# Squares through PSUM, FFN 0's and FFN 1's first superblock in a pinned order, and an own place for the forget bias

## The chip, the cores and the metric

The kernel runs on one core of a Trainium2 chip. The metric is device time in microseconds (us): the median of several executions, smaller is better. Besides the executions that are only timed, one is profiled; the rows shown are from that one. The engines are named as the profile names them: PE (TensorE, the matrix products), DVE (VectorE), ACT (ScalarE), POOL (GpSimd) and SP (SyncE, whose queue issues the DMAs). L276 is line 276 of the kernel before.

## The reference

One step of a two-layer encoder over 1024 prompt frames and 64 sample frames (T = 1088 columns here), with caches of 256 frames. Layer 0 mixes with two kinds of attention (A, B), layer 1 with a forgetting attention (C) and a recurrent branch (D); each layer ends in a SwiGLU feed-forward net.

```python
for layer in range(DEPTH):
    hp = rmsnorm(yp, norm_mix_g[layer])
    mp = ab_mixer(...) if layer % 2 == 0 else cd_mixer(...)
    yp = yp + mp
    yp = yp + swiglu(rmsnorm(yp, norm_ffn_g[layer]), w1, w3, w2)   # (silu(h @ w1) * (h @ w3)) @ w2
y = rmsnorm(yp, final_g)

def rmsnorm(x, g):
    return x * lax.rsqrt(jnp.mean(x * x, axis=-1, keepdims=True) + EPS) * g

def cd_mixer(...):                     # in part
    logf = log_sigmoid(cf + c_f_bias)
    F = jnp.cumsum(logf, axis=1)       # the forget bias of fox_core
    s = q @ k + F[query] - F[key]      # softmax, then times v
    u = causal_conv(dx); h = rg_lru(u) # recurrent branch, out = h * gelu(dg)
```

The same is computed for the sample frames, with the caches in front.

## The kernel before

All data are float32. A product is made of three matmuls on parts of the operands, high x high, high x low and low x high; `split` (L218) makes the parts: ACT copies the high part (L219), DVE or POOL subtracts it for the low part (L220). Activations lie transposed, 128 features on the partitions and the 1088 columns in three chunks (384, 384, 320). On chip there is one array `arena`, addressed by offsets whose names begin with F_, one array `split_arena` for split operands, and `banks`, the eight PSUM banks of 512 columns, which rings hand out in turn.

The engines' programs are static. The order on each engine is set by a scheduler that takes the instructions in the order of the code and weighs what is ready; `issue_after(x)` makes an instruction stand behind x. Each engine runs its list in order, and one that waits holds up all that are behind it. The stages that matter here:

*The output projection (`wout`, L824).* Per chunk, pairs of feature rows are multiplied (L248), added to x on DVE (L850), and squared into a running sum for the norm: `addsq` (L268) squares on ACT (L276) into a small buffer of the arena and adds on DVE (L277). `rms` (L252) multiplies the sum by a matrix of 1/1024 on PE (L258), and ACT takes the root as exp(-0.5 ln). `norm_x` (L906) scales eight rows per chunk on DVE (L910). The steps of `fill_x` (L917), lists `one` and `two` for the two halves of the columns, then make the sums and differences (L944) and the split operands of the feed-forward net, on ACT and DVE.

*The first products of the feed-forward net (`ffn`, L1049; `superblock`, L1012).* A superblock is a 2x2 block product in seven products (as Strassen does it) of 24 matmuls (L1028); there are 22 superblocks. Superblock 0 runs in two rounds, one for each half of the columns, with 12 matmuls a product. `left` (L969) makes the weight side: four adds on POOL (L982 to L985) and seven splits. ACT copies one product out of its bank (L1032) and computes Silu (L1090); DVE adds products (L1036, L1038, L1089).

*The second products and the tail.* Products L1128 to L1130, added to x (L1165), squared through `addsq`; here the adds of the squares go to DVE and POOL in turn. Weights are split on POOL.

*Layer CD (`recurrent`, L1385).* For four blocks m of the recurrent branch: products, a convolution on DVE (L1309, L1311), gates (L1334 to L1337), Gelu (L1293 to L1301) and the scan of the recurrence (`d_close`, L1339: POOL L1349, then ACT, then DVE), stored to `o_spill`. Between them lie the products of the first query heads (`put_q`, L321: ACT L324 and L325, DVE L329) and keys. `forget` (L1237) sums the log forget values with two scans on DVE (L1244) and stores them to `forget_rows`. Later `bias_c` (L761) loads one row of it to all partitions and POOL adds a mask (L765; L741 adds masks to pieces); the attention's first steps (L472) add it to the scores (L460, L461).

## Time and profile before

| | before |
|---|---|
| median of 3 runs | 2751.93 us (2747.84 to 2753.0) |
| the profiled execution | 2753.34 us |
| its span, first to last instruction | 2751.6 us |
| mean granted clock of TensorE | 0.976 |

A row of a timeline gives the start and the length in us, the engine, the line, what is written and read, and in square brackets how long the engine had stood idle before it and whom it waited for. A row of the waits names who waited for whom, how long in all, how often and the longest. The granted clock is a share of full speed.

### The profile page before, as it was taken

How to read it: one execution, taken by the hardware profiler on the slowest of the kernel's cores; microseconds unless marked ns; L12 is line 12 of the kernel's file. 1: busy time of each engine (PE TensorE's matmuls, PEld its weight loads, DVE VectorE, ACT ScalarE, POOL GpSimd, SP SyncE). 2: the span in 40 equal slices, each digit the busy share in tenths (PEclk: the TensorE clock that was granted, in tenths of full speed). 3: DMA queues.
4: the chain of work that ended last, by engine and by line, in shares of the span. 5: the costliest groups of instructions: out<-in, count | busy, mean ns of one | idle time of the engine just before them, and what ended most of it. 6: DMA issues, size and time to landing. Idle time of an engine off the chain costs nothing. (4 is left out here: it accounts for less than half of the span.)

```text
span 2751.6 us, 45123 instructions
## 1 busy us (share of the span) xinstructions
PE 2614.3 (95%) x17614; PEld 2541.5 (92%) x17614; DVE 1353.8 (49%) x2741; ACT 1209.4 (44%) x2384; POOL 1223.8 (44%) x968
## 2 busy tenths in 40 slices
PE   6999999989899999999998979998989999999997
PEld 5899999888899999999988979988989999999997
DVE  7666666667432332422156657777753233242214
ACT  5666667764323233311145566776432323331113
POOL 5222222323766676421364433343377666642123
PEclk9999999999999999999999989999989999999998
DMA  6222222352222212442242442244222222243213
GB/s 204 71 68 78 68 65 61 107 160 68 79 87 79 87 63 87 148 141 71 65 128 49 51 94 75 77 126 157 79 80 100 65 87 68 82 162 127 71 48 106
DMA packets 116407, 253.75 MB, mean 92 GB/s; under 512 B 21577, under 2 KB 70993, under 8 KB 116193
## 3 DMA queue, kind: packets, MB, share of 16 engines
q1 hardware_dynamic: 116192, 250.87, 30.0%
q8 instruction: 138, 2.26, 0.3%
q14 instruction: 77, 0.62, 0.1%
HBM read 182.63 MB, written 65.43 MB: 90 GB/s over the span
## 5 line engine op out<-in xcount | busy, mean ns | idle before, releaser
L220 POOL TENSOR_TENSOR split_arena<-arena,split_arena 128x512 fp32r<-128x512 f32 (+5 forms) x510 | 798.1, 1569 | 1196.9 <-ACT split_arena L219 1121.6
L1028 PE MATMUL banks<-split_arena 128*128 128x272 f32 x7392 | 947.5, 291 | 29.0 <-DVE split_arena L220 12.1
L1028 PEld LDWEIGHTS banks<-split_arena 128*128 128x128 f32 x7392 | 941.8, 191 | 34.1 <-DVE split_arena L220 13.5
L219 ACT ACTIVATE split_arena<-arena 128x512 fp32r<-128x512 f32 (+8 forms) x673 | 469.9, 710 | 1054.2 <-PE banks L1028 439.5
L248 PE MATMUL banks<-split_arena 128*128 128x384 f32 (+1 forms) x3384 | 641.3, 336 | 5.6 <-ACT arena L1337 3.1
L248 PEld LDWEIGHTS banks<-split_arena 128*128 128x128 f32 x3384 | 565.4, 192 | 13.7 <-ACT arena L1337 3.4
L1128 PE MATMUL banks<-split_arena 128*128 128x384 f32 (+1 forms) x1056 | 347.0, 329 | 6.3 <-DVE arena L1095 4.3
L1130 PE MATMUL banks<-split_arena 128*128 128x384 f32 (+1 forms) x1056 | 346.8, 329 | 5.9 <-POOL split_arena L220 5.9
L1129 PE MATMUL banks<-split_arena 128*128 128x384 f32 (+1 forms) x1056 | 346.5, 328 | 0.0
L220 DVE TENSOR_TENSOR split_arena<-banks,split_arena 128x512 fp32r<-128x512 f32 (+4 forms) x312 | 167.4, 541 | 95.7 <-ACT split_arena L219 92.9
L1128 PEld LDWEIGHTS banks<-split_arena 128*128 128x128 f32 x1056 | 199.9, 189 | 7.5 <-issue 3.8
L1130 PEld LDWEIGHTS banks<-split_arena 128*128 128x128 f32 x1056 | 200.0, 189 | 7.1 <-POOL split_arena L220 7.1
L472 DVE CUSTOM_DVE_ANT_0 arena<-banks,arena 128x384 f32<-128x384 f32 (+4 forms) x368 | 175.3, 493 | 56.6 <-PE banks L461 38.4
L1129 PEld LDWEIGHTS banks<-split_arena 128*128 128x128 f32 x1056 | 200.0, 189 | 0.5 <-DVE split_arena L220 0.2
L220 DVE TENSOR_TENSOR split_arena<-arena,split_arena 128x1088 fp32r<-128x1088 f32 (+8 forms) x163 | 161.4, 1001 | 76.8 <-ACT split_arena L219 76.0
L219 ACT ACTIVATE split_arena<-banks 128x512 fp32r<-128x512 f32 (+4 forms) x312 | 146.8, 477 | 98.5 <-PE banks L577 46.0
L1036 DVE TENSOR_TENSOR arena<-banks,arena 128x544 f32<-128x544 f32 (+1 forms) x46 | 32.0, 698 | 300.3 <-PE banks L1028 300.3
L474 ACT ACTIVATE arena<-arena 128x640 f32<-128x640 f32 (+8 forms) x216 | 156.3, 724 | 53.1 <-DVE arena L472 51.7
L1147 DVE TENSOR_TENSOR arena<-banks,arena 128x384 f32<-128x384 f32 (+1 forms) x96 | 51.3, 534 | 258.5 <-PE banks L1130 258.3
L577 PE MATMUL banks<-arena 128*128 128x128 f32 (+2 forms) x828 | 135.1, 275 | 16.6 <-DVE arena L493 10.1
L577 PEld LDWEIGHTS banks<-arena 128*128 128x128 f32 (+2 forms) x828 | 96.4, 141 | 34.6 <-DVE arena L493 13.6
L236 PE MATMUL banks<-split_arena 128*128 128x384 f32 (+1 forms) x312 | 107.2, 345 | 16.2 <-DVE split_arena L329 9.6
(165 smaller groups left out, 3128.7 us busy)
## 6 DMA issues: line engine op xcount, KB each, us to landing
arena<-in_w_dram SPq DMA_DIRECT2D x120, 512.0 KB, 3.5
h_spill<-arena SPq DMA_DIRECT2D x22, 1088.0 KB, 4.2
arena<-h_spill SPq DMA_DIRECT2D x44, 544.0 KB, 4.8
arena<-in_abw_dram SPq DMA_DIRECT2D x24, 512.0 KB, 3.9
arena<-in_w_dram SPq DMA_DIRECT2D x28, 384.0 KB, 3.2
arena<-in_cdw_dram SPq DMA_DIRECT2D x20, 512.0 KB, 3.8
x_spill<-arena SPq DMA_DIRECT2D x48, 192.0 KB, 2.3
arena<-x_spill SPq DMA_DIRECT2D x16, 544.0 KB, 4.6
```

The source lines that it names most:

```text
L219: self.nc.scalar.activation(hi, x, AF.Copy)
L220: return sub.tensor_tensor(lo, x, hi.bitcast(F32), op=ALU.subtract)
L236: nc.tensor.matmul(ps, wh[:, k], hh[k][:, c0:c0 + n], start=(k == ks[0]), stop=False)
L248: self.pe = self.nc.tensor.matmul(ps, x[:, k], y[k][:, c0:c0 + n], start=a and i == 0, stop=z and i == 2).ins
L472: nc.vector.tensor_tensor_reduce(o, p, t, -1.0, low, ALU.add, ALU.min, to)
L474: nc.scalar.activation(sb, sb, AF.Exp, bias=st[:, 0:1], scale=-1.0, accum_out=st[:, 1:2])
L577: nc.tensor.transpose(pt[:r, t * nq + s * m:t * nq + s * m + m], src, self.ident[:m, :m])
L1028: nc.tensor.matmul(bank[:, p], l[:, k], r[:, k, x], start=first and i == 0, stop=k == 3 and i == 2, skip_group_check=True)
L1128: nc.tensor.matmul(ps, wh, h[:, c0:c0 + n], start=j == j0, stop=False)
L1129: nc.tensor.matmul(ps, wh, lo[:, c0:c0 + n], start=False, stop=False)
L1130: nc.tensor.matmul(ps, wl, h[:, c0:c0 + n], start=False, stop=j == j1 - 1)
L1147: nc.vector.tensor_tensor(xs, ps, xs, op=ALU.add)
```

## The change

It has five parts.

1. For chunks 1 and 2 of `wout`, and in the feed-forward net's tail, the squares go to a PSUM bank, and all adds are DVE's. In the tail the last chunk no longer has two running sums, so its mean square is one matmul instead of two.
2. `norm_x(0)` is issued behind the first pair of products of chunk 1.
3. The mean square and scaling of chunk 2 and the last steps of `fill_x` move into superblock 0 (`rest` behind the third product of round 1, `last` behind the seventh). The products of superblock 0 stand in a pinned order, 0, 2, 1, 3, 4, 5, 6 in each round; Silu in it comes behind the root of the mean square. The weights of superblock 1 are loaded later, and `left(1)` may be issued only behind the high part of the last fill.
4. The log forget values have a place of their own (F_LF) instead of two slots of the recurrent branch, and `forget` stands behind the convolution of m = 1 in the code.
5. The bias row of head 0 is loaded into that place after m = 2; the buffer `stg2` has one slot instead of two.

```diff
 F_X = (6144, 3072, 9216)
-F_ACC = (12928, 11776, 12160)
-F_TMP = (13312, 13696, 12544)
+F_ACC = (12928, 11776, 12544)
+F_TMP = (13312, 13696, 12160)
 F_RB = 14080
...
-F_STG2 = 15232
+F_LF = 14464
+F_STG2 = 15808
...
+        self.sq = None
...
     def split(self, hi, lo, x, sub):
-        self.nc.scalar.activation(hi, x, AF.Copy)
-        return sub.tensor_tensor(lo, x, hi.bitcast(F32), op=ALU.subtract)
+        self.hi = self.nc.scalar.activation(hi, x, AF.Copy).ins
+        lo = sub.tensor_tensor(lo, x, hi.bitcast(F32), op=ALU.subtract)
+        self.lo = lo.ins
+        return lo
...
-        nc.scalar.activation(r, r, AF.Exp, scale=-0.5)
+        self.after_rms = nc.scalar.activation(r, r, AF.Exp, scale=-0.5).ins
...
+            s = (self.sq or self.tmp).get()[:, :n]
             nc.scalar.activation(s, xap, AF.Square)
             (add or nc.vector).tensor_tensor(acc, acc, s, op=ALU.add)
...
-        t = self.v(F_BIAS + 1344 * (h % 2), 1344)
+        t = self.v(F_BIAS + 1344 * (h % 2) if h else F_LF, 1344)
...
-        self.mm = self.mmf
+        self.mm = self.sq = self.mmf
         ws[0] = weights(0, c)
-        self.norm_x(0, gcol)
         one, two = self.fill_x(0), self.fill_x(1)
         for m in (6, 4, 0, 2):
             yield from products((m, m + 1), ws[m], 1, self.mmf)
             if m == 6:
+                with self.tc.issue_after(self.pe):
+                    self.norm_x(0, gcol)
                 ws[2] = weights(2, b)
             else:
                 one.pop(0)()
             elif m == 0:
                 self.ops = [next(first) for _ in range(3)]
                 one.pop(0)()
-                two.pop(0)()
             elif m == 2:
                 self.ops += list(first)
-                one.pop(0)()
-        self.tmp = self.tmp3
-        r = self.rms(2)
-        one.pop(0)()
-        self.norm_x(2, gcol, r)
-        one.pop(0)()
-        for f in two:
-            f()
+                two.pop(0)()
+        self.sq = None
+        def rest():
+            self.mm = Ring(self.PS, [3584], 512)
+            r = self.rms(2)
+            self.mm = self.mmf
+            for f in one:
+                f()
+            self.norm_x(2, gcol, r)
+        def last():
+            for f in two:
+                f()
+            return self.hi
+        self.fill = rest, last
...
-        adds.tensor_tensor(s1, a21, a22, op=ALU.add)
-        adds.tensor_tensor(a21, a11, a21, op=ALU.subtract)
-        adds.tensor_tensor(a11, s1, a11, op=ALU.subtract)
-        adds.tensor_tensor(a12, a12, a11, op=ALU.subtract)
+        with self.tc.issue_after(self.lo):
+            adds.tensor_tensor(s1, a21, a22, op=ALU.add)
+            adds.tensor_tensor(a21, a11, a21, op=ALU.subtract)
+            adds.tensor_tensor(a11, s1, a11, op=ALU.subtract)
+            adds.tensor_tensor(a12, a12, a11, op=ALU.subtract)
...
         for rnd in rounds:
             z = slice(rnd[0], rnd[-1] + 1)
-            for j, bank in enumerate((a, a, e, b, c, a, a)):
+            for j in (0, 2, 1, 3, 4, 5, 6) if hooks else range(7):
+                bank = (a, a, e, b, c, a, a)[j]
                 wh, wl = ops[j]
                 th, tl = T_[j]
                 for p in rnd:
                     x = slice(HB * p, HB * p + HB)
-                    for k in range(4):
-                        first = k == 0 and j not in (1, 6)
-                        for i, (l, r) in enumerate(((wh, th), (wh, tl), (wl, th))):
-                            nc.tensor.matmul(bank[:, p], l[:, k], r[:, k, x], start=first and i == 0, stop=k == 3 and i == 2,
-                                             skip_group_check=True)
+                    with self.tc.issue_after(last.ins) if hooks and last else contextlib.nullcontext():
+                        for k in range(4):
+                            first = k == 0 and j not in (1, 6)
+                            for i, (l, r) in enumerate(((wh, th), (wh, tl), (wl, th))):
+                                last = nc.tensor.matmul(bank[:, p], l[:, k], r[:, k, x], start=first and i == 0,
+                                                        stop=k == 3 and i == 2, skip_group_check=True)
+                if hooks and j == 1 and rnd is rounds[0]:
+                    with self.tc.issue_after(last.ins):
+                        hooks[0]()
...
+                    if hooks and rnd is rounds[0]:
+                        hooks[1]()
...
-        raws = {1: self.raws(1)}
+        raws, filled = {}, []
         ops = self.ops
+        def rest():
+            filled.append(self.fill[1]())
+            raws[1] = self.raws(1)
...
-            def use_1(name, z, ps, add, to, g=g):
+            def use_1(name, z, ps, add, to, g=g, s=s):
                 o = g[:, int(name[0]) - 1, z, int(name[1]) - 1, :]
                 if add is not None:
                     nc.vector.tensor_tensor(o, ps, add, op=ALU.add)
-                nc.scalar.activation(o, ps if add is None else o, AF.Silu)
+                with self.tc.issue_after(self.after_rms) if s == 0 else contextlib.nullcontext():
+                    nc.scalar.activation(o, ps if add is None else o, AF.Silu)
...
-            nxt, got = None, []
-            if s + 1 < NB:
-                nxt = self.left(*raws.pop(s + 1), nc.gpsimd, nc.gpsimd)
+            nxt, got = [], []
             def then(j, s=s, nxt=nxt, got=got):
-                if nxt is not None:
-                    got.append(next(nxt))
+                if s + 1 < NB:
+                    if j == 0:
+                        nxt.append(self.left(*raws.pop(s + 1), nc.gpsimd, nc.gpsimd))
+                    with self.tc.issue_after(filled[0]) if s == 0 else contextlib.nullcontext():
+                        got.append(next(nxt[0]))
                     if j == 3 and s + 2 < NB:
...
+            self.superblock(s, ops, ((0,), (1,)) if s == 0 else ((0, 1),), use_1 if s % 2 == 0 else use_3, then, (self.fill[0], rest) if s == 0 else None)
...
+        self.sq = self.mmf
         for q, (i, cs) in enumerate(uses):
...
-                    self.addsq(ci, m, xs, (nc.vector, nc.gpsimd)[m % 2])
-                elif q < 11:
-                    self.addsq(2, m, xs, nc.vector, first=q == 8)
-                else:
-                    self.addsq(2, m, xs, (nc.gpsimd, nc.vector)[q % 2], 2 - 2 * (q % 2), q == 11)
+                self.addsq(ci, m, xs, first=q == (0, 0, 8)[ci])
...
+        self.sq = None
         def rest():
-            r = self.rms(2, [2, 0], self.v(F_END + 384, 384))
+            r = self.rms(2, to=self.v(F_END + 384, 384))
...
-        rest = [self.D.get() for _ in range(2)]
-        Lf = self.v(F_S, 1344)[0:8]
+        Lf = self.v(F_LF, 1344)[0:8]
...
-        self.forget(Lf)
-        self.D.put(*rest)
-        stg, self.stg2 = self.stg, Ring(self.M, [F_STG2, F_STG2 + 384], 384)
...
+            if m == 1:
+                self.forget(Lf)
+            elif m == 2:
+                self.bias0 = self.bias_c(0)
             b = nb
...
-        self.units([("C", lambda u=u: [self.bias_c(2 * u + j) for j in range(2)], units[u]) for u in range(4)],
+        self.units([("C", lambda u=u: [self.bias0 if 2 * u + j == 0 else self.bias_c(2 * u + j) for j in range(2)], units[u]) for u in range(4)],
```

Where it moves instructions. First ScalarE ahead of the mean square of chunk 0 (L276 is now L281, L219 is L222): squares, splits of other rows (320) and of weights (1024). Before:

```order
L276 ACTIVATE arena<-arena 128x384
L219 ACTIVATE split_arena<-arena 128x320 x6
L276 ACTIVATE arena<-arena 128x384
L219 ACTIVATE split_arena<-arena 128x1024
L276 ACTIVATE arena<-arena 128x384
L273 ACTIVATE arena<-arena 128x384
L219 ACTIVATE split_arena<-arena 128x1024
L276 ACTIVATE arena<-arena 128x384
```

and now:

```order
L222 ACTIVATE split_arena<-arena 128x320 x7
L281 ACTIVATE arena<-arena 128x384 x2
L222 ACTIVATE split_arena<-arena 128x1024
L278 ACTIVATE arena<-arena 128x384
L222 ACTIVATE split_arena<-arena 128x1024
L281 ACTIVATE banks<-arena 128x384
L179 ACT_TABLE_LOAD
L267 ACTIVATE arena<-banks,arena 128x384
```

The last two squares of chunk 0 stand together ahead of both weight splits; behind them the squares go to banks, and there is a table load ahead of the logarithm.

Second TensorE from the chunk 1 products of `wout` on (L258, now L263, is the mean square; L1028, now L1046, the superblocks). Before:

```order
L248 MATMUL banks<-split_arena 128x384 x132
L248 MATMUL banks<-split_arena 128x320 x16
L258 MATMUL banks<-arena 128x384
L248 MATMUL banks<-split_arena 128x320 x176
L1028 MATMUL banks<-split_arena 128x272 x28
L258 MATMUL banks<-arena 128x320
L1028 MATMUL banks<-split_arena 128x272 x3644
```

and now:

```order
L253 MATMUL banks<-split_arena 128x384 x138
L253 MATMUL banks<-split_arena 128x320 x17
L263 MATMUL banks<-arena 128x384
L253 MATMUL banks<-split_arena 128x320 x175
L1046 MATMUL banks<-split_arena 128x272 x36
L263 MATMUL banks<-arena 128x320
L1046 MATMUL banks<-split_arena 128x272 x3636
```

The mean square of chunk 0 (ahead of the first row) has 138 of the 192 matmuls of chunk 1 behind it instead of 132; that of chunk 2 comes after 36 matmuls of superblock 0 instead of 28.

Third GpSimd in layer CD, behind the weight splits (L1294 is now L1322, L1349 is L1377, L765 is L770, L741 is L746). Before:

```order
L220 TENSOR_TENSOR split_arena<-arena,split_arena 128x1024 x2
L1294 TENSOR_SCALAR arena<-arena 128x384
L1269 MEMSET arena 128x3
L1294 TENSOR_SCALAR arena<-arena 128x384
L1349 TENSOR_TENSOR arena<-arena 128x384 x2
L1349 TENSOR_TENSOR arena<-arena 128x256
L1349 TENSOR_TENSOR arena<-arena 128x64
L1294 TENSOR_SCALAR arena<-arena 128x320
```

and now:

```order
L223 TENSOR_TENSOR split_arena<-arena,split_arena 128x1024 x2
L1322 TENSOR_SCALAR arena<-arena 128x384 x2
L770 TENSOR_TENSOR arena<-arena 64x64
L746 TENSOR_TENSOR arena<-arena 128x128 x3
L1377 TENSOR_TENSOR arena<-arena 128x384 x2
L1377 TENSOR_TENSOR arena<-arena 128x256
L1377 TENSOR_TENSOR arena<-arena 128x64
L1322 TENSOR_SCALAR arena<-arena 128x320
```

The memset that stood between the two L1294 is gone from here, and the mask add on the bias row of head 0 (L770) and three mask adds (L746) stand ahead of the four operations of the recurrence (L1377).

8 lines of the change are left out of this document (4 added, 4 removed).

## Prediction

> **What bounds the kernel now.** I read the page's first part for the bound, then TensorE's waits, then TensorE's timeline and windows where those waits are long. The first row is the page's; the others are TensorE's waits: line, what released it, us in total, times, longest.
>
> ```profile
> PE 2614.3 (95%) x17614; PEld 2541.5 (92%) x17614; DVE 1353.8 (49%) x2741; ACT 1209.4 (44%) x2384; POOL 1223.8 (44%) x968
> ...
> PE banks L258 <- DVE arena L277: 17.2, 3, 10.4
> PE banks L1028 <- DVE split_arena L220: 12.1, 6, 6.0
> ...
> PE banks L236 <- DVE split_arena L329: 9.6, 2, 8.4
> PE banks L1028 <- ACT split_arena L219: 9.0, 3, 6.5
> PE banks L460 <- DVE arena L472: 8.0, 1, 8.0
> ```
>
> TensorE is busy for 2614.3 of the 2751.6 us of the span, so the kernel gains only where TensorE stands idle (137.3 us in all), or runs at a low clock behind such a stand. The change leaves the products as they are; it can take away waits and add waits. The longest of those above lie at its places, apart from the 10.4 us at the start of the program. I call them place 1 (the first mean square and the first two superblocks of FFN 0), place 2 (the recurrent part up to the first items of the fox attention) and place 3 (the same superblocks of FFN 1).
>
> What a stand costs beyond itself is seen in windows of 4 us (the columns are sum, PE, PEld, DVE, ACT, POOL, granted clock, DMA share, GB/s):
>
> ```profile
> 1500.00:1504.00 4.00, 4.00 (x14) 4.00 (x13) 3.11 (x5) 1.01 (x3) 2.64 (x3) 0.50 0.20 55
> 1504.00:1508.00 4.00, 4.00 (x26) 4.00 (x26) 0.82 (x3) 3.97 (x8) 0.00 (x0) 0.97 0.01 2
> 1536.00:1540.00 4.00, 2.79 (x16) 2.70 (x16) 3.92 (x5) 3.00 (x7) 3.63 (x3) 1.00 0.53 53
> ```
>
> After the stand of 8.42 us that ends at 1499.04 the clock is 0.50 for about 4 us: 14 matmuls where the next window has 26, so some 2 us are lost. In the window of the stand of 1.21 us before 1537.31 the clock stays 1.00. I put 2 us on every stand above 3 us and nothing on a shorter one. The Trainium skill (TensorE: Matmul & The Clock Gate, Part 1, "What's actually happening") has a gate that goes to half rate after at least one idle window of about 3.4 us. By that rule some stands between 3 and 4 us stay warm; if instead every new stand below cooled the clock, that would cost 2 us more for each of four short stands, 8 us in all.
>
> **Place 1, the first mean square.** TensorE, VectorE and GpSimd around 611 us:
>
> ```profile
> 616.18 1.65 PE L258 MATMUL banks<-arena 128*128 128x384 f32 x2 [5.87 <-DVE arena L277]
> 611.11 5.49 DVE L277 TENSOR_TENSOR arena<-arena 128x384 f32<-128x384 f32 x3 [0.35 <-ACT arena L276]
> 610.75 4.97 POOL L220 TENSOR_TENSOR split_arena<-arena,split_arena 128x1024 fp32r<-128x1024 f32 x2 [26.21 <-ACT split_arena L219]
> 624.73 1.08 DVE L850 TENSOR_TENSOR arena<-banks,arena 128x384 f32<-128x384 f32 x2 [0.16 <-PE banks L248]
> ```
>
> Three adds of squares, whose inputs both lie in the arena, take 5.49 us while GpSimd splits weights; an add of the same size that reads a bank (L850) takes 0.54. After the change the last squares of chunk 0 stand on ScalarE ahead of the weight split that feeds GpSimd, so the adds should end at about 612 and not 616.2; but TensorE reaches L258 54 matmuls into chunk 1 instead of 60, about 1 us sooner. The wait falls from 5.87 to about 2.5, below the point where the clock drops: 3.4 + 1.1 for part of the cold stretch, **4.5 us** (2 to 6).
>
> **Place 1, superblocks 0 and 1.** The order before and now is shown with the change.
>
> ```profile
> 677.04 0.60 PE L1028 MATMUL banks<-split_arena 128*128 128x272 f32 x1 [6.02 <-DVE split_arena L220]
> ...
> 710.00 0.82 PE L1028 MATMUL banks<-split_arena 128*128 128x272 f32 x2 [6.48 <-ACT split_arena L219]
> ...
> 713.85 66.39 PE L1028 MATMUL banks<-split_arena 128*128 128x272 f32 x520 [0.32 <-DVE arena L1089]
> 687.69 3.79 DVE L910 SCALAR_TENSOR_TENSOR arena<-arena 128x320 f32<-128x320 f32 x8 [0.78 <-ACT arena L265]
> 695.66 8.38 POOL L220 TENSOR_TENSOR split_arena<-arena,split_arena 128x512 fp32r<-128x512 f32 x1 [21.83 <-ACT split_arena L219]
> 704.01 1.26 POOL L982 TENSOR_TENSOR arena<-arena 128x512 f32<-128x512 f32 x1
> ```
>
> A product takes 66.39 / 520 = 0.128 us, and each superblock has 168 of them. The first starts at about 670.7 (6.02 and a few tenths before 677.04); at 713.85 some 169 are left, so both end near 735.4: 64.7 us for 43 us of work, the rest waits and cold clock. Now through the new order. *The third product* waits for ScalarE's copy out of the first one's bank, which stands behind the last two squares: 1.8. *The seventh*: from the mean square on TensorE has three products, 4.6 us; meanwhile ScalarE needs some 1.1 for the root, and VectorE the eight scalings (3.79) and six short operations of about 0.4 before the add (L1089) that frees the bank: 7.3, so 2.7 of waiting. *Round 2*: VectorE's remaining fills are the 11.91 us of the third busy time in this window, less 0.4 of the scalings:
>
> ```profile
> 691.00:703.00 12.00, 10.55 (x69) 10.01 (x70) 11.91 (x17) 7.92 (x11) 7.34 (x1) 0.86 0.14 45
> ```
>
> All but the last 1.8 of them stand ahead of what round 2's fourth product reads: 9.7 against four products, 6.1: 3.6. *Superblock 1*: the chain `left(1)` may now start only after the last fill's hi split, about 28 us in, at 698.7. One split beside VectorE (until 702.3), another, four adds of 1.26 and a split and a copy on ScalarE end at 710; TensorE is there at 704.7: 5.3. Together 13.4, and 2 us of cold clock beyond what the mean of 0.128 holds: 43 + 15.4 = 58.4, a gain of **6 us** (0 to 12).
>
> **Place 3** has the same code (its first mean square waited less). Its longest stand:
>
> ```profile
> 1981.36 0.77 PE L1028 MATMUL banks<-split_arena 128*128 128x272 f32 x4 [3.86 <-POOL split_arena L220]
> ```
>
> It is smaller than layer 0's, but there are more of them; the new order is that of layer 0, and so is the work, so I take the same **6 us** (0 to 12).
>
> **Place 2.** Here the diff and the order part ways. In the code `forget()` comes later, but on VectorE its two scans still stand where they stood, ahead of the convolution of m = 1. What moves is that nothing waits for their store any more, and that the bias row of head 0 is loaded at once.
>
> ```profile
> 1499.04 0.69 PE L236 MATMUL banks<-split_arena 128*128 128x384 f32 x1 [8.42 <-DVE split_arena L329]
> 1484.55 5.16 DVE L1244 TENSOR_TENSOR_SCAN arena<-arena 8x1024 f32<-8x1024 f32 x2 [0.24 <-DMA out_c_logfT_dram<-arena]
> 1496.00 0.56 DVE L1295 TENSOR_TENSOR arena<-arena 128x384 f32<-128x384 f32 x1 [2.66 <-POOL arena L1294]
> 1495.28 0.10 POOL L1269 MEMSET arena<- 128x3 f32 x1 [5.25 <-DMA forget_rows<-arena]
> 1497.28 4.71 POOL L1349 TENSOR_TENSOR arena<-arena 128x384 f32<-128x384 f32 x4 [1.30 <-ACT arena L1337]
> ```
>
> The 2.66 us that VectorE waited behind GpSimd's memset go: TensorE resumes at 1496.4 instead of 1499.0. But GpSimd's queue now has, in front of the four L1349, the mask add on the bias row (L765) and three L741. The row is loaded only when the store of `forget_rows`, which landed at 1495.28, has landed. How long such a load takes is seen in the DMA view (the median of issue to landing where it was measured) and in one load's issue and landing:
>
> ```profile
> arena<-forget_rows SPq DMA_DIRECT2D x2, 672.0 KB, 12.6
> ...
> 1627.58 0.32 SPq L172 DMA_DIRECT2D arena<-forget_rows  x1
> 1632.83 0.31 POOL L765 TENSOR_TENSOR arena<-arena 64x64 f32<-64x64 f32 x1 [6.26 <-DMA arena<-forget_rows]
> 1633.11 1.29 POOL L741 TENSOR_TENSOR arena<-arena 128x128 f32<-128x128 f32 x3
> ```
>
> From its issue at 1627.58 to GpSimd's start at 1632.83 it is 5.25 us, and 12.6 where a large store and a weight load go beside it. I take 5.25, since the store of the rows has just drained. L1349 starts at 1495.3 + 5.3 + 0.3 + 1.3 = 1502.2, 4.9 us later than before, and the recurrent chain behind it with it. Who waits for that chain:
>
> ```profile
> 1520.24 0.33 SPq L172 DMA_DIRECT2D o_spill<-arena  x1
> 1531.53 0.10 POOL L1269 MEMSET arena<- 128x3 f32 x1 [12.79 <-DMA o_spill<-arena]
> 1534.70 0.56 DVE L1295 TENSOR_TENSOR arena<-arena 128x384 f32<-128x384 f32 x1 [5.71 <-POOL arena L1294]
> 1537.31 0.45 PE L236 MATMUL banks<-split_arena 128*128 128x384 f32 x1 [1.21 <-DVE split_arena L329]
> 1627.16 0.80 PE L460 MATMUL banks<-split_arena 128*128 128x512 f32 x1 [7.98 <-DVE arena L472]
> ```
>
> Its result is stored to `o_spill`, GpSimd waits for the landing, VectorE for GpSimd, and TensorE for the bank that VectorE holds. All of it 4.9 us later: TensorE resumes at 1542.2 instead of 1537.3, after a stand of about 9 us, and loses 2 us to the clock: **6.9 us late**. The stand of 7.98 us at 1627.16 was the wait for the bias rows; both are then loaded early (head 1 some 15 us sooner), so it goes, with 2 us of cold clock behind it. Net 8.0 + 2 - 6.9 = **3 us** gained; with the load at 12.6 it is 7 us less (-4), with it hidden 7 more (+10). The single slot of `stg2` costs nothing: the uses lie over 8 us apart.
>
> **The FFN's tail.** GpSimd loses the adds of squares, in both layers the 16 of this row and 4 narrower ones:
>
> ```profile
> L277 POOL TENSOR_TENSOR arena<-arena 128x384 f32<-128x384 f32 x16 | 16.9, 1054 | 20.8 <-ACT arena L276 20.8
> 1391.57 0.45 PE L1130 MATMUL banks<-split_arena 128*128 128x384 f32 x1 [1.05 <-POOL split_arena L220]
> ```
>
> VectorE takes them at 0.54 and has idle time between. Weight splits on GpSimd come up to 1 us sooner, two short stands shrink: **1.5 us** (-1 to 4) for layer 0 and **0.5** (0 to 1) for layer 1's end, where stores and the last scalings bound.
>
> **Sum** against the profiled execution (2753.34 us: span 2751.6 and 1.7 around it; 1.4 above the median of the runs, 2751.93): 4.5 + 6 + 6 + 3 + 1.5 + 0.5 = 21.5, so 2731.8; less the 1.4, since a median is predicted, and rounded: **2731**.
>
> **The rivals.**
> *The new queue gives it back.* The superblocks gain nothing in one layer (0 + 6), the bias load takes 12.6 (-4), the tail 0: 4.5 + 6 - 4 = 6.5, so **2746**. For it speaks that each new wait stands in a queue of another engine; against it that both long stands at 677 and 710 lose their cause.
> *VectorE was the bound of the whole stretch.* With adds from banks no longer stretched, its fills come earlier than I put them, and both superblocks gain 11; place 2 hides the bias load (+10): 4.5 + 22 + 10 + 2 = 38.5, so **2714**.
> *The change does not do what it says.* For the scans this is already in the forecast. If the products of superblock 0 also wait as before, only 4.5 + 2 and place 2's 3 less 7 are left: within 0.2%, **2750**.
> *Slower: GpSimd's chain beside VectorE's fills.* Before, one split of 128x512 took 8.38 us at 695.66 while VectorE was busy, while its adds take 1.26 with VectorE idle. The chain `left(1)` now stands wholly behind the fills; if VectorE still works when it starts, three of its operations stretched by 7.1 us cost 21 us per layer. 42 - 21.5 = 20 us slower, **2773**; it decides from 11 us per layer. Against it: VectorE is idle 8.88 us in this place before:
>
> ```profile
> 711.79 0.96 DVE L220 TENSOR_TENSOR split_arena<-arena,split_arena 128x192 fp32r<-128x192 f32 x1 [8.88 <-ACT split_arena L219]
> ```
>
> The Trainium skill (SBUF — State Buffer, "SBUF: two separate sides") has GpSimd and VectorE lock a shared port for a whole instruction; the 8.38 us span many VectorE instructions, so here the loser waits longer than for one.
>
> **How the numbers follow.** Forecast (gain 12 to 33) 0.60, given back 0.12, everything hidden 0.12, no effect 0.09, slower 0.07. The measurement tells about 0.2% (5.5 us) from no change. Faster by more: 0.60 + 0.12 + 0.12 = 0.84; within: 0.09; slower: 0.07. The range, 2712 to 2748, holds the forecast and the first two rivals, 0.84 together, and leaves out 0.16; the bounds of place 2 and of the superblocks reach further only where they all fall on one side.
>
> **What would show it.** Right: after 670 us no stand before the first product of superblock 0, four stands of 1.5 to 5.5 us in the superblocks; GpSimd's L765 at 1500 to 1502 on before's clock, a stand of about 9 us near 1537 and none near 1620. Wrong: GpSimd splits over 5 us after 698, a bias load above 8 us, or a new stand where the sample items of the fox attention begin.

## The result and the profile after

| | before | changed |
|---|---|---|
| median, runs taken side by side | 2749.89 us (4 runs, 2747.45 to 2753.0) | 2724.64 us (4 runs, 2723.0 to 2726.12) |
| ratio, 95% interval | | 0.9907 (0.9890 to 0.9925) |
| span of the profiled execution | 2751.6 us | 2721.2 us |

The change makes the kernel 25.3 us faster by the medians; 21 were forecast, and 2724.6 lies in the range of 2712 to 2748. The two profiled spans differ by 30.4 us, since the profiled execution is the slowest of its runs for the kernel before and the fastest for the changed one. The changed kernel's lines are numbered anew: L263 is the mean square on TensorE (L258 before), L1046 the superblock's product (L1028), L222 and L223 the two halves of a split (L219, L220), L281 and L282 a square and its add (L276, L277), L334 was L329, L1053 (L1032) is the copy of a superblock's first product, L855 (L850) adds a product to x.

The changed kernel's page, first part, and its waits of TensorE:

```profile
PE 2601.7 (96%) x17610; PEld 2528.7 (93%) x17610; DVE 1341.5 (49%) x2763; ACT 1201.6 (44%) x2382; POOL 1171.1 (43%) x948
...
PE banks L263 <- DVE arena L282: 12.3, 3, 10.5
...
PE banks L241 <- DVE split_arena L334: 9.6, 2, 5.2
PE banks L1046 <- DVE arena L282: 7.8, 1, 7.8
PE banks L1046 <- ACT arena L1053: 7.4, 3, 3.5
```

Of before's rows, L460 behind L472 (8.0) is gone and L1028 behind VectorE's L220 (12.1) has shrunk to 1.9. L1046 behind L1053 (7.4, before 0.3) is among the stands that were forecast; a single wait of 7.8 us of a superblock's product behind the add of a square was not. To see where the 30.4 us lie I take the start of the same instruction in both timelines:

| mark | before | changed | gain since the last mark | forecast |
|---|---|---|---|---|
| first mean square, layer 0 | 616.18 | 607.38 | 8.8 | 4.5 |
| ScalarE's first copy in superblock 3 | 760.51 | 744.88 | 6.8 | 6 |
| first gate (L1334, L1362) of layer CD | 1481.4 | 1467.1 | -1.3 | 1.5 |
| last gate | 1590.4 | 1575.0 | 1.1 | |
| first transpose of the weights in the fox attention (L577, L582) | 1628.94 | 1603.44 | 10.1 | 3 with the row above |
| its last | 1920.1 | 1889.8 | 4.8 | 0 |
| ScalarE's first copy in superblock 3, layer 1 | 2064.90 | 2033.96 | 0.6 | 6 |
| end of the span | 2751.6 | 2721.2 | -0.5 | 0.5 |

That the sum was near is in part luck: the terms of the first mean square, of place 2 and of the fox attention were too small, and those of place 3 and the tail too large. Not all of the 8.8 us arose at the first mean square: the same product of chunk 1, shortly ahead of it, starts at 608.07 before and at 606.27 in the changed kernel, and another shortly behind it at 620.89 and 611.26. A lead of 1.8 us was there already, and the place gained 7.8. The first three rows of the changed kernel's timeline are layer 0's mean square, the others the new stand in layer 1:

```profile
605.29 1.17 ACT L281 ACTIVATE arena<-arena 128x384 f32<-128x384 f32 x2
607.38 0.91 PE L263 MATMUL banks<-arena 128*128 128x384 f32 x2
607.50 4.74 POOL L223 TENSOR_TENSOR split_arena<-arena,split_arena 128x1024 fp32r<-128x1024 f32 x2 [24.58 <-PE banks L253]
...
1945.21 1.72 ACT L222 ACTIVATE split_arena<-arena 128x512 fp32r<-128x512 f32 x3 [2.47 <-POOL arena L999]
1950.27 0.87 DVE L855 TENSOR_TENSOR arena<-banks,arena 128x320 f32<-128x320 f32 x2
1950.78 0.84 ACT L281 ACTIVATE banks<-arena 128x320 f32<-128x320 f32 x2 [1.50 <-DVE arena L855]
1953.40 0.47 DVE L282 TENSOR_TENSOR arena<-arena,banks 128x320 f32<-128x320 f32 x1
1953.93 6.25 PE L1046 MATMUL banks<-split_arena 128*128 128x272 f32 x36 [7.84 <-DVE arena L282]
```

At the mean square GpSimd's split now starts when TensorE has already begun, and nothing is stretched. In layer 1 the first product of superblock 0 waits for the whole path of the last square: VectorE's L855, the square into PSUM, VectorE's add. The same code had no such stand in layer 0.

### The profile page after: what moved, and what is told of

Read it like the earlier page. It is cut to its first block, busy times and chain, and to the rows that moved or that the text cites. A ratio compares the mean times of both kernels' runs of the same rounds, so it can differ in the third digit from the quotient of the medians.

```text
span 2721.2 us, 44951 instructions
## 1 busy us (share of the span) xinstructions
PE 2601.7 (96%) x17610; PEld 2528.7 (93%) x17610; DVE 1341.5 (49%) x2763; ACT 1201.6 (44%) x2382; POOL 1171.1 (43%) x948
## 4 chain that ended last, share of the span: by engine, by line
PE 75%; DVE 7%; ACT 5%; issue 4%; DMA 4%; POOL 4%; SPq 0%; DVEq 0%; ACTq 0%; POOLq 0%
PE banks L1046 32%; PE banks L253 15%; PE banks L1160 6%; PE banks L1159 6%; PE banks L1158 6%; PE banks L582 3%; POOL split_arena L223 2%; ACT split_arena L222 2%; DVE split_arena L223 2%; PE banks L465 2%; PE banks L466 1%; PE banks L507 1%; PE banks L508 1%; DMA arena<-o_spill 1%; DVE arena L291 1%
## 5 line engine op out<-in xcount | busy, mean ns | idle before, releaser
L223 POOL TENSOR_TENSOR split_arena<-arena,split_arena 128x512 fp32r<-128x512 f32 (+5 forms) x510 | 773.9, 1529 | 1241.2 <-ACT split_arena L222 1141.2
L1046 PE MATMUL banks<-split_arena 128*128 128x272 f32 x7392 | 946.4, 290 | 29.8 <-DVE arena L282 7.8
L1046 PEld LDWEIGHTS banks<-split_arena 128*128 128x128 f32 x7392 | 939.2, 190 | 36.9 <-DVE arena L282 8.1
L222 ACT ACTIVATE split_arena<-arena 128x512 fp32r<-128x512 f32 (+8 forms) x673 | 465.8, 709 | 1028.4 <-PE banks L1046 300.3
L223 DVE TENSOR_TENSOR split_arena<-banks,split_arena 128x512 fp32r<-128x512 f32 (+4 forms) x312 | 167.6, 541 | 89.6 <-ACT split_arena L222 87.0
L223 DVE TENSOR_TENSOR split_arena<-arena,split_arena 128x1088 fp32r<-128x1088 f32 (+8 forms) x163 | 156.6, 969 | 70.7 <-ACT split_arena L222 69.9
L222 ACT ACTIVATE split_arena<-banks 128x512 fp32r<-128x512 f32 (+4 forms) x312 | 146.6, 476 | 94.3 <-PE banks L582 41.2
L582 PE MATMUL banks<-arena 128*128 128x128 f32 (+2 forms) x828 | 133.5, 273 | 15.8 <-DVE arena L498 9.8
L582 PEld LDWEIGHTS banks<-arena 128*128 128x128 f32 (+2 forms) x828 | 95.1, 139 | 34.2 <-DVE arena L498 13.6
L241 PE MATMUL banks<-split_arena 128*128 128x384 f32 (+1 forms) x312 | 106.2, 342 | 16.0 <-DVE split_arena L334 9.6
```

Source lines behind the costliest of these rows:

```text
L222: self.hi = self.nc.scalar.activation(hi, x, AF.Copy).ins
L223: lo = sub.tensor_tensor(lo, x, hi.bitcast(F32), op=ALU.subtract)
L241: nc.tensor.matmul(ps, wh[:, k], hh[k][:, c0:c0 + n], start=(k == ks[0]), stop=False)
L582: nc.tensor.transpose(pt[:r, t * nq + s * m:t * nq + s * m + m], src, self.ident[:m, :m])
L1046: last = nc.tensor.matmul(bank[:, p], l[:, k], r[:, k, x], start=first and i == 0, stop=k == 3 and i == 2, skip_group_check=True)
```

## The experiments

All are edits of the changed kernel. Each ratio is to the kernel before on the same chip; the interval is in brackets. The changed kernel itself was run once more for comparison.

| run | median us | ratio |
|---|---|---|
| after_again | 2721.53 | 0.9904 (0.9887 to 0.9920) |
| ring_first | 2714.05 | 0.9880 (0.9866 to 0.9893) |
| ring_second | 2729.04 | 0.9935 (0.9922 to 0.9947) |
| norm_early | 2732.52 | 0.9946 (0.9933 to 0.9958) |
| sb_before | 2716.52 | 0.9890 (0.9877 to 0.9904) |
| ring_sb | 2716.88 | 0.9892 (0.9875 to 0.9909) |
| squares_arena | 2731.16 | 0.9938 (0.9926 to 0.9951) |
| bias_late | 2722.47 | 0.9911 (0.9897 to 0.9924) |
| bias_place | 2733.09 | 0.9941 (0.9928 to 0.9955) |
| lf_slots | 2731.28 | 0.9946 (0.9933 to 0.9958) |
| tail_pinned | 2723.27 | 0.9916 (0.9901 to 0.9930) |
| copy_first | 2707.51 | 0.9853 (0.9836 to 0.9869) |

> The changed kernel once more, on the chip of the two runs beside it. All theories: 0.989 to 0.9925 of the kernel before. By the theory of the held bank its stand in front of superblock 0 of layer 1 is 7 to 8 us again, and the one in front of layer 0's below 1. If the fox attention's gain of some 4 us was chance (a stand of 3.62 us in the kernel before that cooled the clock, 2.87 in the changed one that didn't), that stand stays below 3.2 here, or comes back with the cold clock.

The stand in layer 1 was 7.32 us, the one in the fox attention 1.44.

### Why layer 1 gained nothing: the ring of banks

The squares take their banks from the ring that also serves the products (mmf, eight banks in turn), and the ring runs on from stage to stage. Counted through the code, the output projection's chunk 1 begins at bank 0 in layer 0 and at bank 1 in layer 1. So, by this count, the last two squares lie in banks 6 and 7 in layer 0, in 7 and 0 in layer 1; and bank 0 is where superblock 0's first product goes. Two runs set the ring by hand.

```diff
         self.mm = self.sq = self.mmf
+        self.mmf.i = 0        # ring_first; 1 in ring_second
         ws[0] = weights(0, c)
```

> The changed kernel with one line more: the ring of PSUM banks is set to its first bank where the output projection's second chunk begins, in both layers. Layer 0 is there already, layer 1 was one bank further. Theory (held bank): in the changed kernel the last square of layer 1 lies in bank 0, which the first product of superblock 0 writes, so that product waits 7.84 us until VectorE has added the square; in layer 0 the last square lies in bank 7, and nothing waits. Then with this line the stand goes in layer 1, the cold clock behind it too, and the superblocks of layer 1 take about the 481.6 us of layer 0 instead of 492.3: 8 to 11 us faster than the changed kernel, 2714 to 2717 us, ratio to the kernel before 0.987. Rival (late weights): the weights of superblock 0 landed 3 us later in layer 1 than in layer 0; then a stand of 4 us or more stays in front of its first product, put down to GpSimd or the weight load, and the time is 2721 to 2725.

> The same line with the second bank instead of the first: layer 1 stays as it is, layer 0 gets the place that layer 1 has. Theory (held bank): now the last square of layer 0 lies in bank 0 as well, and its superblock 0 begins with a stand of 5 to 8 us behind VectorE's add, with a cold clock behind it: 6 to 10 us slower than the changed kernel, 2731 to 2735 us. Rival (late weights): layer 0's weights come early, so nothing changes: 2723 to 2726.

TensorE's timeline in ring_first, layer 1 (the line numbers are one higher):

```profile
1935.84 7.35 PE L253 MATMUL banks<-split_arena 128*128 128x320 f32 x49
1943.02 1.68 PE L1047 MATMUL banks<-split_arena 128*128 128x272 f32 x12
1945.14 0.52 PE L1047 MATMUL banks<-split_arena 128*128 128x272 f32 x2 [0.44 <-DVE arena L282]
```

and in ring_second, layer 0 and layer 1:

```profile
670.10 6.33 PE L1047 MATMUL banks<-split_arena 128*128 128x272 f32 x36 [5.86 <-DVE arena L282]
...
1958.69 1.73 PE L1047 MATMUL banks<-split_arena 128*128 128x272 f32 x6 [7.97 <-DVE arena L282]
```

One number moves the stand: with bank 0 free layer 1 starts without it, with bank 0 held layer 0 has it too. The late weights are not the cause. The time followed: 0.0025 of the kernel's time, some 7 us (8 to 11 were expected), is won by the one, some 8 lost by the other.

### What the new order of superblock 0 is worth

sb_before puts the code of the third part back (the tail of `wout`, `ffn`, `superblock` and `left` as before); ring_sb is the same with ring_first's line.

```diff
-            for j in (0, 2, 1, 3, 4, 5, 6) if hooks else range(7):
+            for j in range(7):
...
-        def rest():
-            self.mm = Ring(self.PS, [3584], 512)
             r = self.rms(2)
...
-        self.fill = rest, last
```

> The changed kernel with its third part undone: mean square, scaling and fills of chunk 2 stand ahead of superblock 0 again, its products are not pinned, and the weights of superblock 1 come early; squares through PSUM and the rest stay. Theory (order): layer 0 loses the 6 us that its superblocks gained; layer 1, where the part gained nothing behind its held bank, stays within 3: 2729 to 2735 us. Rival (squares): the adds from PSUM made that gain, and the order of the superblock none; then 2722 to 2727.

> Third part undone (as in sb_before) and the ring of banks set to its first bank in both layers (as in ring_first). In sb_before alone layer 1's ring began two banks further, so its last two squares lay in other banks than in the changed kernel, and that run doesn't separate bank and order. Beside ring_first, this one differs in the third part alone, and no square holds the first product's bank in either. Theory (bank): the new order of superblock 0 is worth little, 0 to 4 us in each layer, and what sb_before gained over the changed kernel was the bank: 2713 to 2721 us, ratio to before 0.988 to 0.990. Rival (order costs): the new order itself makes layer 1 late, and without it the kernel is 4 us or more faster than ring_first: 2710 or less. Rival (order gains, as forecast): without it both layers lose 6 us each: 2725 or more.

sb_before came out against both theories: without the third part the kernel is not slower but, by its ratio, as fast as ring_first. In it layer 1's ring began at bank 2, hence ring_sb, whose time is the one that its first theory named. To compare stage by stage I take the time from the start of chunk 1's mean square to ScalarE's first copy in superblock 3:

| | layer 0 | layer 1 |
|---|---|---|
| before | 116.3 | 114.5 |
| changed, after_again | 110.3, 110.4 | 114.4, 116.1 |
| ring_first | 106.2 | 109.5 |
| sb_before | 109.9 | 108.7 |
| ring_sb | 109.9 | 111.1 |
| copy_first (below) | 105.1 | 105.8 |

(Before, layer 0: 644.17 to 760.51; changed: 634.54 to 744.88; the others likewise.) With the old order layer 0 takes 6.5 us less than before, as much as with the new one. So the 6.8 us of layer 0 are not the order's alone. What the order itself is worth can't be told: ring_first is 3.6 and 1.6 us shorter than ring_sb in the two layers, but in layer 0 ring_first is the same code as the changed kernel, and over seven runs of that code (the changed kernel twice, ring_first, bias_late, bias_place, lf_slots, tail_pinned) the stretch took 106.2 to 110.4 us. By the time of the whole kernel the two can't be told apart either. (In ring_sb a stand of 3.05 us remains in front of layer 1's first product; its cause was not followed.)

Where the old order's 6.5 us come from is seen on VectorE, which has the same list here in before and in sb_before. The first three rows are before's, the others those of sb_before (its own line numbers: L1039 is the superblock's product, L989 the first add of `left`):

```profile
653.53 2.69 DVE L277 TENSOR_TENSOR arena<-arena 128x320 f32<-128x320 f32 x1
666.20 1.58 DVE L277 TENSOR_TENSOR arena<-arena 128x320 f32<-128x320 f32 x1
669.53 1.58 DVE L277 TENSOR_TENSOR arena<-arena 128x320 f32<-128x320 f32 x1
...
646.63 0.47 DVE L282 TENSOR_TENSOR arena<-arena,banks 128x320 f32<-128x320 f32 x1
657.80 0.47 DVE L282 TENSOR_TENSOR arena<-arena,banks 128x320 f32<-128x320 f32 x1
659.63 0.47 DVE L282 TENSOR_TENSOR arena<-arena,banks 128x320 f32<-128x320 f32 x1
665.27 0.52 PE L1039 MATMUL banks<-split_arena 128*128 128x272 f32 x2 [1.21 <-DVE arena L282]
680.00 6.40 POOL L989 TENSOR_TENSOR arena<-arena 128x512 f32<-128x512 f32 x1 [12.21 <-DMA arena<-in_w_dram]
693.35 5.61 PE L1039 MATMUL banks<-split_arena 128*128 128x272 f32 x27 [8.62 <-ACT split_arena L222]
```

Three adds with the square in a bank take 4.4 us less than with it in the arena, and the first of before's two long stands shrinks by 4.8 us, from 6.02 to 1.21. The second, 6.48 us before, stays with the old order (8.62): there GpSimd's add takes 6.40 us beside VectorE's fills instead of 1.26. The run meant to take the squares out of PSUM again was spoilt:

```diff
-        self.mm = self.sq = self.mmf
+        self.mm = self.mmf
```

> The changed kernel with the output projection's squares of chunks 1 and 2 in the arena again (those of the tail still go through PSUM). Theory (held bank): no square holds a bank, so layer 1's stand of 7.84 us in front of superblock 0 goes; the adds run beside GpSimd's chain again (1.5 us instead of 0.5 each), which makes the mean square of chunk 2 up to 4 us late: 2 to 8 us faster than the changed kernel, 2716 to 2723. Rival (relief): without PSUM VectorE falls so far behind in both layers that the superblocks lose 3 us or more each: 2728 to 2736.

The first product of superblock 0 in layer 0, in its timeline:

```profile
668.78 6.87 PE L1046 MATMUL banks<-split_arena 128*128 128x272 f32 x36 [5.95 <-DVE arena L855]
```

Without squares in it the ring stands elsewhere: by the count, the last pair of products itself lies in banks 0 and 1 of layer 0, and the stand of 5.95 us is the wait for VectorE to add that product (L855). The held bank again, by another tenant; and VectorE comes to that add later than in the changed kernel, since adds of squares take 1.58 us again. The two are mixed in this stand. In layer 1 the stand in front of superblock 0 is gone, as the first theory had it (the stretch of the table takes 110.3 us), and in layer 0 the stretch takes 113.7. The time of the whole kernel fits the rival, but what PSUM relieves is not measured cleanly by this run.

### The first mean square

```diff
+        self.norm_x(0, gcol)
         one, two = self.fill_x(0), self.fill_x(1)
...
             if m == 6:
-                with self.tc.issue_after(self.pe):
-                    self.norm_x(0, gcol)
```

> The changed kernel with its second part undone: the scaling of chunk 0 is issued ahead of the products of chunk 1 again. By the order on ScalarE the hi split of a weight then stands again between the last two squares of chunk 0. Theory (order): the gain of 8 us at the first mean square is this order alone, since chunk 0's squares lie in the arena in both kernels; the adds of squares run beside GpSimd's split again, a stand of 4 to 6 us stands again in front of the first mean square of layer 0, and the kernel is 5 to 8 us slower than the changed one: 2730 to 2733. Rival (PSUM): the squares in PSUM relieve the shared path and made that gain; then this changes nothing, 2723 to 2726.

The timeline of norm_early around its first mean square:

```profile
606.27 4.96 POOL L223 TENSOR_TENSOR split_arena<-arena,split_arena 128x1024 fp32r<-128x1024 f32 x2 [24.71 <-ACT split_arena L222]
606.63 5.01 DVE L282 TENSOR_TENSOR arena<-arena 128x384 f32<-128x384 f32 x2 [0.35 <-ACT arena L281]
611.70 1.65 PE L263 MATMUL banks<-arena 128*128 128x384 f32 x2 [5.39 <-DVE arena L282]
```

The stand is back with the order on ScalarE: one split among the squares starts GpSimd 0.4 us ahead of two adds, which then take 5.01 us together instead of 0.55 each. The squares of chunks 1 and 2 go through PSUM in this run as in the changed kernel, so PSUM has no part in this stand. By the ratios the run is some 11 us slower than the changed kernel, more than the 5 to 8 expected.

### The bias row and the forget values

bias_late takes out the early load of head 0's row but keeps its new place; bias_place puts the row back into its old place as well; lf_slots puts the log forget values back into two slots and leaves the row.

```diff
-            elif m == 2:
-                self.bias0 = self.bias_c(0)          # bias_late, bias_place
...
-        t = self.v(F_BIAS + 1344 * (h % 2) if h else F_LF, 1344)
+        t = self.v(F_BIAS + 1344 * (h % 2), 1344)    # bias_place
...
-        Lf = self.v(F_LF, 1344)[0:8]
+        rest = [self.D.get() for _ in range(2)]      # lf_slots
+        Lf = self.v(F_S, 1344)[0:8]
...
         self.gate_weights()
+        self.forget(Lf)
+        self.D.put(*rest)
```

> The changed kernel, but the bias row of head 0 is loaded where it was loaded before, with head 1's (into the new place). Theory (early load): the stand of about 8 us at the first fox scores (behind VectorE's bias add) comes back with its cold clock, +8 to +10; in the recurrent part GpSimd no longer has the mask adds and their wait for the load ahead of its products, which gives back 1 to 3: 2729 to 2734. Rival (own place): the own place of the log forget values and the later store are what gained there, and the early load nothing: 2722 to 2726.

The edit moved nothing: the scheduler issues the load 2.0 us behind the store of the rows (1477.31 after 1475.29), as in the changed kernel, since the place is free. Where the call stands in the code does not matter here, and the run decides between neither theory, since the early load is still there.

> The changed kernel with its fifth part undone whole: the bias row of head 0 goes to its old place again, which lies in the slots of the recurrent branch, and is loaded with head 1's. Theory (place): the load can be issued only when the last block's slots come free, so the stand of about 8 us in front of the first scores of the fox attention comes back, with 2 us of cold clock; GpSimd loses the mask adds (1.6 us) and their wait in the recurrent part, which gives back 1 to 3: 2730 to 2735. Rival (earlier chain): that stand is gone since the recurrent chain as a whole ends earlier, and it doesn't return: 2720 to 2725.

TensorE's timeline in bias_place:

```profile
1481.64 0.44 PE L241 MATMUL banks<-split_arena 128*128 128x384 f32 x1 [2.14 <-DVE split_arena L334]
...
1612.71 0.69 PE L465 MATMUL banks<-split_arena 128*128 128x384 f32 x1 [5.71 <-DVE arena L477]
```

As the theory has it: the load cannot go before the last block's slots are free, the stand at the first scores returns (5.71 us), and near 1480 the stand is 2.14 us against 4.30 in after_again.

> The changed kernel with its fourth part undone: the log forget values lie in two slots of the recurrent branch again, and the scans stand there in the code; the bias row of head 0 still has its own place and is loaded early. Theory (store): GpSimd's memset of a slot waits for the store of the forget rows again, VectorE behind it and TensorE behind VectorE, so the stand near 1479 us grows from 4.4 to 7 or 8: 3 to 6 us slower than the changed kernel, 2728 to 2731. Rival (load): what GpSimd waits for is the load of the bias row in either kernel, which comes after that store, so the store costs nothing more: 2722 to 2726.

GpSimd's and TensorE's rows of the timeline of lf_slots:

```profile
1467.70 0.10 POOL L1297 MEMSET arena<- 128x3 f32 x1 [2.80 <-DMA forget_rows<-arena]
1471.66 0.44 PE L241 MATMUL banks<-split_arena 128*128 128x384 f32 x1 [2.50 <-DVE split_arena L334]
...
1602.72 0.31 POOL L770 TENSOR_TENSOR arena<-arena 64x64 f32<-64x64 f32 x1 [6.67 <-DMA arena<-forget_rows]
1603.82 0.42 PE L508 MATMUL banks<-split_arena 128*128 128x64 f32 x1 [5.67 <-DVE split_arena L223]
```

The sign was as the theory said, the reason was not, and the loss was larger than its 3 to 6 us: some 11 by the ratios. The memset waits for the store, yet the stand it was to lengthen is short (2.50). The loss is at the second head: its row is loaded at 1590.82, in after_again at 1582.43, which is 11.4 us later if both are counted from the tail's end (1424.8 and 1427.8). Slots are handed out first in, first out. With the two slots taken, by the code's count the last block draws slot 7 for its gate, and head 1's row lies over slots 6 and 7; with an own place for the forget values the last block draws 5, and 7 is free one block earlier.

### The tail, and a better version

> The changed kernel with the feed-forward net's tail as before: its squares in the arena, added on VectorE and GpSimd in turn, and two running sums for the last chunk. So that nothing else moves, the ring of banks is set to the changed kernel's place at the start of layer CD and of layer 1's second chunk. Theory (forecast): the tail loses 1.5 us in layer 0 and 0.5 in layer 1, 2 us slower than the changed kernel: 2725 to 2728. Rival (trace of the changed kernel, where the tail was 1.5 us longer than before): the adds on VectorE stand in front of others there, and without them it is 1 to 3 us faster: 2721 to 2724.

0.9916 against 0.9904 on the same chip, with intervals that overlap: the sign is the forecast's, but neither it nor the size is certain.

In ring_first the longest stand left in the superblocks was that behind the copy of superblock 1's first product (L1054), which stands on ScalarE behind weight splits that wait for GpSimd. copy_first is ring_first with those splits issued behind the copy (the places that hand over `more` and wait for `put_hi` are left out):

```diff
                     for p in rnd:
-                        nc.scalar.activation(u[:, p], a[:, p], AF.Copy)
+                        copy = nc.scalar.activation(u[:, p], a[:, p], AF.Copy)
+                    with self.tc.issue_after(copy.ins):
+                        ops.extend(more)      # the last five splits of left(1), in superblock 1
+                    self.put_hi = self.hi     # left(2) is issued behind them
```

> ring_first with one order more: ScalarE's two copies of superblock 1's first product stand ahead of the last five weight splits of left(1), which before stood in front of them and waited for GpSimd's chain. Theory (ScalarE's queue): in ring_first TensorE stands 2.80 us in both layers behind that copy alone (the product is done at about 697, the copy starts at 700.4); with the copy ahead both stands go, and what comes next, the low part of the third operand, is ready before the third product: 4 to 6 us faster than ring_first, ratio to before 0.986, 2708 to 2710 us. Rival (chain): GpSimd's chain is itself the bound there, TensorE gets one product further and then stands 2 to 3 us behind the split: 2713 to 2715, as ring_first.

TensorE's timeline at this place in ring_first:

```profile
700.87 9.42 PE L1047 MATMUL banks<-split_arena 128*128 128x272 f32 x73 [2.80 <-ACT arena L1054]
```

and TensorE's and ScalarE's in copy_first:

```profile
691.40 12.80 PE L1047 MATMUL banks<-split_arena 128*128 128x272 f32 x86 [0.93 <-DVE split_arena L223]
700.84 0.40 ACT L1054 ACTIVATE arena<-banks 128x272 f32<-128x272 f32 x1
702.40 0.40 ACT L1054 ACTIVATE arena<-banks 128x272 f32<-128x272 f32 x1 [1.16 <-PE banks L1047]
702.74 1.67 ACT L222 ACTIVATE split_arena<-arena 128x512 fp32r<-128x512 f32 x3
```

The stand is gone and none takes its place. At 0.9853 this is the fastest version: 2707.5 us, about 14 us ahead of the changed kernel by the ratios and with an interval that lies wholly below its. Ahead of ring_first it is by some 7 us, and there the two intervals just overlap. (The profiled execution is the slowest of the four, 2713.08 us.)

## Why the prediction was right, and where it was not

*The bound* held: the products are the same, TensorE's busy time fell by 12.6 us at a mean granted clock of 0.987 instead of 0.976, and nearly all of the gain lies at the places named.

*First mean square* (4.5; 8.8 in the trace, 7.8 of them at this place): the mechanism was right, and norm_early shows it. The mis-sized term is "the adds should end at about 612": on the changed kernel's own clock they ended at 607.3, on before's at about 609, since the squares are ahead of the split far enough for no add to run beside GpSimd. The wait was 0 and not 2.5, and with it went all of the cold stretch, some 2 us and not 1.1.

*Superblocks of layer 0* (6; 6.8): right in size, partly wrong in reason, and the size is in part luck. The four stands came where they were worked out, only shorter: 1.14, 2.56, 1.48 with 0.93, and 3.51 us, 9.6 in all against 13.4. In return the clock cost more than the 2 us put on it: it stood at 0.50 for three stretches of 3.41 us, which can cost up to half of that, 5.1 us. The two errors nearly cancel. And the old order with squares in PSUM gains the same. The step that failed takes both of before's long stands as what the old order costs: the first (6.02) hung on adds of squares stretched beside GpSimd, and those went by another part of the change; only the second stays with the old order.

*Place 3* (6; 0.6): the step that failed is "the new order is that of layer 0, and so is the work, so I take the same". Code and order are the same, the ring's position isn't, and it decided which product waits for the last square. This is the one path that the forecast had wrong outright, and it cost the change most: setting the ring gives about 7 us. Behind the stand the work did gain what was forecast: from its first product the 336 of the two superblocks take 65.1 us before, 57.2 in the changed kernel and 59.4 in after_again. The stand of 7.84 in front took it.

*Place 2* (3; 11.2): "Net 8.0 + 2 - 6.9" had the first two terms right in total (10.1). The step that failed is the third, "6.9 late": up to the last gate the changed kernel gained 1.1. The second of TensorE's two stands did grow, but to 5.17 us and not 9, and the first shrank from 8.42 to 4.38. These rows of the changed kernel's timeline show why:

```profile
1473.12 0.27 SPq L175 DMA_DIRECT2D forget_rows<-arena  x1
1475.15 0.34 SPq L175 DMA_DIRECT2D arena<-forget_rows  x1
1479.21 0.31 POOL L770 TENSOR_TENSOR arena<-arena 64x64 f32<-64x64 f32 x1 [4.99 <-DMA arena<-forget_rows]
1480.74 2.93 POOL L1377 TENSOR_TENSOR arena<-arena 128x384 f32<-128x384 f32 x4
1478.77 0.45 PE L241 MATMUL banks<-split_arena 128*128 128x384 f32 x1 [4.38 <-DVE split_arena L334]
1520.20 0.59 PE L241 MATMUL banks<-split_arena 128*128 128x384 f32 x1 [5.17 <-DVE split_arena L334]
```

I took 4.5 us from the store's issue to the load's, and 5.25 for the load; they were 2.0 and 4.1. GpSimd's products (L1377, L1349 before) started 16.5 us ahead of before where the clock of the stage was 14.3 ahead: 2.2 earlier, not 4.9 later. The reason that I gave for the gain was half of it: the early row needs its own place (bias_place), but the forget values' place also frees head 1's slot (lf_slots). That the scans would stay where they were was right.

*The tail* (1.5; -1.3 in the trace; 1.7 by the medians of tail_pinned and after_again) stays open: over the runs with the new tail the stretch of that row takes 719.5 to 724.0 us, 720.9 before and 723.6 in tail_pinned. *The fox attention* (0; 4.8): about 3 us of it are one stand, 3.62 us long with the clock at 0.50 behind it in the kernel before, 2.87 with the clock at 1.00 in the changed one, 1.44 in after_again. In nine of the experiments it is 1.39 to 1.46 us, so the short one is the rule in the changed kernel. Of before there is only one profile, so whether its 3.62 is the rule or chance stays open.

*The rivals.* The slower one (GpSimd's chain stretched beside VectorE's fills) did not come: `left(1)`'s adds took 1.28 us each. Of "VectorE was the bound of the whole stretch" one part came: place 2 hid the load, and its +10 measured 11.2. The 11 us for the superblocks of each layer did not come.

*Two smaller things.* The sum, 2731.8 less 1.4, rounds to 2730 and not 2731. And the rule "2 us on every stand above 3 us and nothing on a shorter one" is not borne out: the clock also fell behind the stand of 2.56 us above (see the last section).

## What to carry to other kernels

Where one ring serves several stages, count its position at each place where a fixed bank follows: the same code in a second layer may meet another bank, and whoever holds it last sets the start. Ask of a load that is moved which memory it waits for, before asking where its call stands. And after a forecast by stands, undo each part alone: what one part of a change is given credit for may be another part's work.

## What was not expected of the hardware

Whether a stand cools the clock is not a matter of its length alone. In ring_first TensorE stands 2.80 us behind the same copy in both layers, and only in layer 1 does the clock fall. The granted clock is the third number from the end, PE's busy time the first behind the comma; two windows of layer 0 and the next, then two of layer 1:

```profile
696.29:699.70 3.41, 1.78 (x15) 1.56 (x13) 0.00 (x0) 1.78 (x4) 3.41 (x4) 1.00 0.00 0
699.70:703.12 3.42, 2.25 (x18) 2.25 (x19) 0.00 (x0) 2.44 (x6) 3.42 (x4) 1.00 0.00 0
703.12:706.53 3.41, 3.41 (x30) 3.41 (x29) 0.72 (x1) 0.00 (x0) 3.41 (x4) 1.00 0.65 208
...
1979.70:1983.11 3.41, 1.16 (x10) 0.93 (x8) 0.00 (x0) 2.09 (x5) 3.41 (x4) 1.00 0.00 0
1983.11:1986.53 3.42, 2.88 (x12) 2.88 (x13) 0.00 (x0) 1.82 (x5) 3.42 (x3) 0.50 0.05 7
```

And the changed kernel around its stand of 2.56 us, which ends at 675.94:

```profile
673.83:677.24 3.41, 1.30 (x10) 1.30 (x11) 3.22 (x8) 2.02 (x4) 0.00 (x0) 1.00 0.49 156
677.24:680.65 3.41, 3.41 (x17) 3.41 (x17) 3.38 (x5) 1.52 (x3) 0.00 (x0) 0.50 0.02 5
680.65:684.06 3.41, 3.09 (x25) 2.87 (x23) 3.16 (x5) 1.68 (x3) 0.00 (x0) 1.00 0.00 0
```

In each trace the clock changes only at steps of 3.41 us: in the changed kernel it is 0.50 from 677.24 to 680.65 and again from 701.13 to 704.54, seven steps later. In layer 0 of ring_first a step's end cuts the stand into 1.63 and 1.17 us, and the clock stays at 1.00; in layer 1 2.25 us of one step are idle, in the changed kernel 2.11, and the next step runs at 0.50. Counted over all fourteen traces from 90 us on, each of the 188 steps at full clock with more than 1.9 us of idle time was followed by one at 0.50, none of the 10249 with less than 1.65 was, and of the 44 between 16 were. So a stand of 2 to 3 us may or may not cool the clock, by how it falls on the steps, and the same code of layer 0 took 106.2 us in one run and 110.4 in another. Where the steps begin differs from trace to trace, so for a kernel this is chance. The Trainium skill (TensorE: Matmul & The Clock Gate, Part 1, "What's actually happening") puts the idle window at about 3.4 us; the steps here have that length, but a step that was idle for 2.11 of its 3.41 us was enough.
